# A two-layer encoder on one core: layer 0's ConvFFN in five groups, half of layer 1's W_out split where it is used, more blocks by seven products

## The chip, the core and the metric

The kernel runs on one core of one Trainium2 chip. The metric is the device time in microseconds of one execution of the whole program. Of the kernel before there are three runs, and one more execution that the hardware profiler recorded.

A core has five engines that run side by side, each through its own list of instructions in order, and that wait for one another by semaphores. PE (TensorE) multiplies matrices, and loads the stationary operand beforehand (PEld). DVE (VectorE) and ACT (ScalarE) do elementwise work, POOL (GpSimd) a little more of it, and SP issues the DMA transfers.

## The reference, cut to what matters

x has 512 positions and 1024 channels, in float32. Each of two layers has a mixing half (a Fourier group and windowed attention, joined by `w_o`) and a ConvFFN with 2816 hidden channels.

```python
mix = jnp.concatenate([rmsnorm(y_f, g_fourier_out[l]), rmsnorm(y_a, g_attn_out[l])], axis=-1)
x = x + mix @ w_o[l]

h = rmsnorm(x, norm2[l])
up = dwconv_centred(h @ w_up[l], conv_w[l], conv_b[l])
gate, val = up[..., :D_FF], up[..., D_FF:]
x = x + (jax.nn.silu(gate) * val) @ w_down[l]
```

`dwconv_centred` is a convolution over three neighbouring positions, channel by channel.

## The kernel before

**Layout and arithmetic.** x lies transposed in eight tiles of 128 channels by 512 positions. A float32 operand of a matmul is split into two halves of a reduced type: `split` lets ACT copy the high half and DVE subtract it from the source, which gives the low half (`wsplit` does it for weights, into the tiles whi and wlo, five buffers of each). `mm3` multiplies high by high, low by high and high by low, so a block product is three matmuls (L124, L125, L126). PSUM has eight banks, shared out by tags.

**The ConvFFN.** The 2816 hidden channels are 22 blocks, `fi` from 0 to 21. A *pair* is the gate block and the value block of one fi. There are two ways to make it. `up_eight` multiplies the eight input tiles one after the other: 2 blocks x 8 products, each of 512 columns. `up_seven` treats two output blocks, the two halves of the input channels and the two halves of the positions as a 2 x 2 matrix of blocks and forms it by seven products in place of eight (Strassen's scheme), each over four tiles and 256 columns. It needs four sums of weight tiles on DVE (into the tile sums and in place in wraw), seven splits in place of four, and more additions of results; the sums of the input are made once a layer (`seven_h`, into the tiles room). `SEVEN[l]` lists the fi that go this way. Then `conv` (one ACT and two DVE instructions a block), silu, the product of gate and value, and its split into `gu`.

**Groups.** `GROUPS[l]` cuts the 22 pairs into groups (first fi, number). When a group's pairs are done, `rows` multiplies its blocks by the fitting slice of W_down: eight output rows m, each with a load, a split, its matmuls in one PSUM bank, and an addition of the result to x on DVE (the *eviction*). These eight rows are a generator that the next group's pairs draw from, spread out by the rule on `want`; the rest is drained at the group's end. In the last group two of the eight rows are held back to stand behind its last pair. A group of more than four loads W_down row by row and splits it in two parts; a smaller one loads two rows at once and splits each in one.

**Prepared weights.** While layer 0's ConvFFN runs, `presplit(1)` prepares weights of layer 1: it loads a piece, folds it if it belongs to the Fourier group (keys u and f), splits it, and stores both halves in DRAM (`kept`); `PIECES[fi]` says how many pieces are drawn at each pair. Layer 1's first half fetches the halves with `fetch`. There are 44 pieces: 16 of W_qkv, 8 of W_in's Fourier columns, 4 of the Fourier weight, 16 of W_out.

**W_out.** `w_o` has two halves of eight blocks, the Fourier group's (half 0) and the attention's (half 1). The products of half 0 are placed among the last attention steps (`issue_after` with `steps`). Layer 0 loads and splits W_out on the spot (`wchunks`), layer 1 fetches both halves.

**The order.** The program is written out once, unrolled; the framework's scheduler then fixes the order on each engine, drawing instructions forward where their operands allow. So instructions of a pair, of the rows and of the pieces are interleaved on DVE and ACT.

Of the kernel before, what the change touches and what calls it, by code (L numbers as in the profile page):

```python
# [16 lines left out]
P = 128  # L17
# [15 lines left out]
RATE, STEP0 = 1, 12  # L33
FFN_BANKS = ("mm", "mm", "mm", "av", "sc", "sc")

GROUPS = ([(0, 4), (4, 4), (8, 4), (12, 3), (15, 3), (18, 4)], [(0, 4), (4, 6), (10, 6), (16, 6)])

PIECES = [1, 1, 2, 1, 2, 2, 2] + [1, 3] * 7 + [3]
SEVEN = ((7, 9, 11, 13, 15, 17, 19), (7, 8, 10, 11, 12, 14, 15, 16, 18, 19, 20, 21))


def encoder_kernel(tc, t):
# [47 lines left out]
    def halves(z):  # L90
        return [z[:, s, :] for s in range(2)]
# [63 lines left out]
    def presplit(l):  # L155

        late = []

        def keep(key, src):
            n = src.shape[-1]  # L160
            two = [temp(n, "tA", F32R) for _ in range(2)]
            with tc.issue_after(pace[0]) if pace[0] is not None else nullcontext():
                act(two[0], src)
            tt(two[1], src, f(two[0]), ALU.subtract)
            kept[key] = [dp.tile([P, n], F32, tag=f"{key}{s}", name=nm("kept")) for s in range(2)]
            store()
            late.append(lambda: [nc.sync.dma_start(o, f(z)) for o, z in zip(kept[key], two)])

        def store():
            while late:  # L170
                late.pop()()

        def cols(src, n, step):
            def load():
                raw = temp(1024, "m4")
                nc.sync.dma_start(raw[:, :n], src)
                return [raw[:, c:c + step] for c in range(0, n, step)]
            return load

        def prepare(kind, raw):  # L180
            if kind == "u":
                return fold_wu(raw)
            return fold_wf(raw) if kind == "f" else raw

        jobs = []
        for grp in (1, 0):
            for kk in range(KT // 2):
                jobs.append((cols(t["w_qkv"][l, grp, kk], 768, 384), [f"qkv{grp}{2 * kk + i}" for i in range(2)]))
        for kk in range(KT // 2):
            jobs.append((lambda kk=kk: load_wu(l, kk, temp(1024, "m4")), [f"u{2 * kk + i}" for i in range(2)]))  # L190
        for j in range(NF):
            jobs.append((lambda j=j: [load_wf(l, j, temp(1024, "m4"))], [f"f{j}"]))
        for half in range(2):
            for mp in range(KT // 2):
                jobs.append((cols(t["w_o"][l, half, :, mp * 1024:(mp + 1) * 1024], 1024, 512),
                             [f"o{half}{2 * mp + i}" for i in range(2)]))
        got = jobs[0][0]()
        for n, (_, keys) in enumerate(jobs):
            for i, key in enumerate(keys):
                keep(key, prepare(key[0], got[i]))  # L200
                if i == len(keys) - 1 and n + 1 < len(jobs):
                    got = jobs[n + 1][0]()
                yield
        store()
        while True:
            yield
# [282 lines left out]
    for l in range(L):  # L489
# [327 lines left out]
            return o  # L817

        def wo(half, mp):
            if l:  # L820
                return [fetch(f"o{half}{2 * mp + i}") for i in range(2)]
            return wchunks(t["w_o"][l, half, :, mp * 1024:(mp + 1) * 1024], 1024)

# [25 lines left out]
        def rows(f0, nf, gu):  # L849

            last = f0 + nf == FT
            for m in range(KT):
                if nf > 4:
                    w = wchunks(t["w_down"][l, m, :, f0 * P:(f0 + nf) * P], nf * P, step=nf * P // 2)
                else:
                    if m % 2 == 0:
                        raw = wtile()[:, :2 * nf * P].rearrange("p (m c) -> p m c", m=2)
                        nc.sync.dma_start(raw, t["w_down"][l, m:m + 2, :, f0 * P:(f0 + nf) * P].rearrange("m p c -> p m c"))
                    w = [wsplit(raw[:, m % 2, :])]
                kw = -(-nf // len(w))  # L860
                nh = 2 if last and l == L - 1 and m == KT - 1 else 1
                for h in range(nh):
                    q0, q1 = h * S // nh, (h + 1) * S // nh
                    nps[0] += 1
                    o = psum(FFN_BANKS[nps[0] % len(FFN_BANKS)])[:, q0:q1]
                    for k in range(nf):
                        mm3(o, [z[:, (k % kw) * P:(k % kw + 1) * P] for z in w[k // kw]],
                            [gu[k][:, s, q0:q1] for s in range(2)],
                            k == 0, k == nf - 1)
                    tt(x[m][:, q0:q1], x[m][:, q0:q1], o, ALU.add)  # L870
                    if last and l == L - 1:
                        nc.sync.dma_start(t["out"][m, :, q0:q1], x[m][:, q0:q1])
                if last and l < L - 1:
                    nxt.append(norm_tile(m, g1[:, l + 1, :], acc))
                yield

        down = iter(())
        for f0, nf in GROUPS[l]:
            gu = []

            todo = KT - 2 if f0 + nf == FT else KT
            done = 0
            for fi in range(f0, f0 + nf):
                ys_ = []
                for z, u in enumerate((up_seven if fi in SEVEN[l] else up_eight)(l, fi, h2, ts, rb2)):
                    ys_.append(conv(l, fi + z * FT, u))

                    n = 2 * (fi - f0) + z
                    want = -(-todo * (n + 2 - n % 2) // (2 * nf)) if n % 2 or n == 0 else done
                    if nf <= 4:  # L890
                        want = done + -(-(todo - done) // (2 * nf - n))
                    for _ in range(want - done):
                        next(down, None)
                    done = want
                if fi in (3, 4):
                    ts.append(seven_h(len(ts), h2, room))
                for _ in range(PIECES[fi]):
                    next(ahead)
                act(ys_[0], ys_[0], AF.Silu)
                tt(ys_[0], ys_[0], ys_[1], ALU.mult)  # L900
                c = fi % (12 if l else 8)
                if c < 4:
                    a = pair("slab")
                elif c < 8:
                    if c % 2 == 0:
                        two = temp(2048, "pT", F32R).rearrange("p (n s q) -> p n s q", n=2, s=2)
                    a = two[:, c % 2]
                else:
                    a = pair("m4")
                split(a[:, 0, :], a[:, 1, :], ys_[0])  # L910
                gu.append(a)
            for _ in down:
                pass
            down = rows(f0, nf, gu)
# [95 lines left out]
```

## Time and profile before

| | |
|---|---|
| median of three runs | 1039.85 us |
| lowest and highest | 1039.72 and 1041.09 us |
| the profiled execution's own time | 1039.14 us |
| its span, first to last instruction | 1037.4 us |
| PE, DVE, ACT busy | 1024.4, 862.5, 545.8 us |
| DMA | 140.15 MB, 42% of 16 engines' time |

The profiled execution is 1.7 us longer than its span; what lies around the span belongs to no engine's instructions. By the stretches of the trace, layer 0's mixing half fills the first 150 us, its ConvFFN lasts to about 520 us, layer 1's mixing half to about 655 us, and its ConvFFN the rest.

How to read the rows: a row of the timeline begins with start and duration, in us, then the engine, the line in the code, the operation, the tiles it writes and reads (buffer numbers left out), their shape, and how many such instructions the row merges. A row of a group has, behind the bar, busy time in us and the mean duration of one in ns, then idle time of that engine ahead of it. A row of the waits has the total in us, how many, and the longest. On DVE and ACT an instruction can begin before the one ahead of it has ended, so that a distance of starts is shorter than a duration. In a fence, a line of three dots marks rows left out.

### The profile page before, as it was taken

Reading aid. Unit: us, or ns where it says so; the run is one execution under the profiler, and the core shown is the slowest. Engines: PE = TensorE matmul, PEld = TensorE weight load, DVE = VectorE, ACT = ScalarE, POOL = GpSimd, SP = SyncE. Lnnn points to the kernel's source line nnn. Section 1 sums busy time; section 2 is a strip of 40 time slices with the busy share of each in tenths; the row PEclk is TensorE's granted clock in tenths of the full one; section 3 lists DMA queues with packets and bytes.
Section 4 is the critical chain, followed back from the end, with each engine's and each line's share of the span. In section 5 each row is a group of like instructions: output and inputs, shape, how many; then the busy total and the mean of one; then the engine's idle time right before and its main releaser. Section 6 shows DMA issues by size and latency. Waiting matters only on the chain.

```text
span 1037.4 us, 16244 instructions
## 1 busy us (share of the span) xinstructions
PE 1024.4 (99%) x5774; PEld 891.1 (86%) x5774; DVE 862.5 (83%) x1747; ACT 545.8 (53%) x1068; POOL 60.6 (6%) x142
## 2 busy tenths in 40 slices
PE   8999999999999999999999999999999999999998
PEld 8887778888888888888899887888888898989987
DVE  8788749799998889999759876396999998999973
ACT  5338736455555455555544595254555555555631
POOL 0004410000000000000000063000000000000000
PEclk9999999999999999999999999999999999999999
DMA  7232122355564546567766422423224232333242
GB/s 275 87 106 72 44 91 82 117 172 179 163 206 145 193 175 204 186 221 231 240 212 200 151 62 84 141 82 102 82 73 137 82 107 85 104 112 101 68 149 85
DMA packets 62341, 140.15 MB, mean 135 GB/s; under 512 B 6450, under 2 KB 20018, under 8 KB 62260
## 3 DMA queue, kind: packets, MB, share of 16 engines
q1 hardware_dynamic: 62260, 139.12, 41.9%
q8 instruction: 45, 0.74, 0.3%
q14 instruction: 36, 0.29, 0.1%
HBM read 116.02 MB, written 23.07 MB: 134 GB/s over the span
## 4 chain that ended last, share of the span: by engine, by line
PE 92%; DVE 5%; ACT 1%; DMA 1%; issue 1%; POOL 0%; DVEq 0%; ACTq 0%
PE ps L124 27%; PE ps L126 27%; PE ps L125 27%; PE ps L122 3%; PE ps L680 2%; PE ps L673 2%; PE ps L661 1%; DVE tF L100 1%; DMA wraw<-in_w_up_dram 1%; DVE wlo L97 1%; DVE tA L665 1%; PE ps L242 1%; PE ps L235 1%; PE ps L621 0%; PE ps L282 0%
## 5 line engine op out<-in xcount | busy, mean ns | idle before, releaser
L94 ACT ACTIVATE whi<-wraw 128x512 fp32r<-128x512 f32 (+1 forms) x323 | 190.7, 603 | 222.2 <-PE ps L126 130.5
L97 DVE TENSOR_TENSOR wlo<-wraw,whi 128x512 fp32r<-128x512 f32 (+1 forms) x331 | 213.1, 657 | 48.6 <-ACT whi L94 47.7
L124 PE MATMUL ps<-act,whi 128*128 128x512 f32 (+1 forms) x692 | 244.9, 355 | 0.0
L125 PE MATMUL ps<-act,wlo 128*128 128x512 f32 (+1 forms) x692 | 244.4, 355 | 0.4 <-DVE wlo L97 0.3
L126 PE MATMUL ps<-act,whi 128*128 128x512 f32 (+1 forms) x692 | 244.1, 354 | 0.0
L125 PEld LDWEIGHTS ps<-act,wlo 128*128 128x128 f32 x692 | 130.6, 189 | 19.4 <-DVE wlo L97 0.9
L124 PEld LDWEIGHTS ps<-act,whi 128*128 128x128 f32 x692 | 130.6, 189 | 18.7
L126 PEld LDWEIGHTS ps<-act,whi 128*128 128x128 f32 x692 | 130.7, 189 | 18.0
L100 DVE SCALAR_TENSOR_TENSOR tF<-tF,pb,tF 128x511 f32<-128x511 f32 x176 | 130.2, 747 | 4.8 <-ACT tF L94 4.6
L97 DVE TENSOR_TENSOR x<-x,ps 128x512 f32<-128x512 f32 (+1 forms) x97 | 64.9, 677 | 34.9 <-PE ps L126 34.5
L124 PE MATMUL ps<-slab,whi 128*128 128x512 f32 (+1 forms) x240 | 93.1, 390 | 0.7 <-ACT whi L94 0.7
L125 PE MATMUL ps<-slab,wlo 128*128 128x512 f32 (+1 forms) x240 | 91.8, 383 | 0.0
L94 ACT ACTIVATE tF<-tF,pb 128x512 f32<-128x512 f32 x88 | 71.1, 810 | 37.7 <-DVE tF L97 37.1
L126 PE MATMUL ps<-slab,whi 128*128 128x512 f32 (+1 forms) x240 | 89.7, 384 | 0.0
L124 PE MATMUL ps<-room,whi 128*128 128x256 f32 x266 | 75.6, 284 | 0.5 <-DVE tF L97 0.2
L125 PE MATMUL ps<-room,wlo 128*128 128x256 f32 x266 | 75.0, 282 | 0.0
L126 PE MATMUL ps<-room,whi 128*128 128x256 f32 x266 | 74.9, 282 | 0.0
L97 DVE TENSOR_TENSOR tF<-ps,rb 128x512 f32<-128x512 f32 (+1 forms) x85 | 52.6, 627 | 15.3 <-ACT rb L94 11.0
L124 PE MATMUL ps<-pT,whi 128*128 128x512 f32 (+1 forms) x148 | 56.9, 384 | 0.0
L125 PE MATMUL ps<-pT,wlo 128*128 128x512 f32 (+1 forms) x148 | 56.8, 384 | 0.0
L126 PE MATMUL ps<-pT,whi 128*128 128x512 f32 (+1 forms) x148 | 56.1, 384 | 0.0
L124 PEld LDWEIGHTS ps<-slab,whi 128*128 128x128 f32 x240 | 45.1, 188 | 9.8 <-ACT whi L94 0.9
(206 smaller groups left out, 1923.9 us busy)
## 6 DMA issues: line engine op xcount, KB each, us to landing
wraw<-in_w_up_dram SPq DMA_DIRECT2D x88, 512.0 KB, 3.8
kept<-tA SPq DMA_DIRECT2D x56, 256.0 KB, 3.2
wraw<-in_w_down_dram SPq DMA_DIRECT2D x32, 384.0 KB, 3.8
wraw<-in_w_down_dram SPq DMA_DIRECT2D x20, 512.0 KB, 4.0
whi<-kept SPq DMA_DIRECT2D x28, 256.0 KB, 3.1
wlo<-kept SPq DMA_DIRECT2D x28, 256.0 KB, 3.0
kept<-tA SPq DMA_DIRECT2D x32, 192.0 KB, 1.9
wraw<-in_w_o_dram SPq DMA_DIRECT2D x8, 512.0 KB, 4.3
```

The lines of the kernel that those rows point to most:

```text
L94: return nc.scalar.activation(out, in_, func, **kw)
L97: return (eng or nc.vector).tensor_tensor(out, a, b, op=op)
L100: return nc.vector.scalar_tensor_tensor(out=out, in0=a, scalar=s, in1=b, op0=op0, op1=op1)
L122: nc.tensor.matmul(out, a[0], b[0], start=start, stop=stop, **kw)
L124: nc.tensor.matmul(out, a[0], b[0], start=start, stop=False, **kw)
L125: nc.tensor.matmul(out, a[1], b[0], start=False, stop=False, **kw)
L126: nc.tensor.matmul(out, a[0], b[1], start=False, stop=stop, **kw)
L235: nc.tensor.matmul(pt[:, 2 * b:2 * b + 2], acc[:, b * P:(b + 1) * P], ones2, start=True, stop=True)
L242: nc.tensor.matmul(pt[:, b * P:(b + 1) * P], r[:, b:b + 1].to_broadcast([P, P]), ident, start=True, stop=True)
L661: nc.tensor.matmul(sc[:, :n], qT[p][:, e, i * P:(i + 1) * P], kT[g][:, s, j0 * P:(j1 + 1) * P], start=s == 0, stop=s == 1)
L673: tr = nc.tensor.transpose(pp[:, j * P:(j + 1) * P], pr[:, j * P:(j + 1) * P], ident)
L680: pv = nc.tensor.matmul(py[64 * e:64 * e + 64, i0 * P:(i1 + 1) * P], vp[:, j, 64 * g:64 * g + 64], pT[:, half, e, b0:b0 + 2 * (i1 - i0) + ...
```

## The change

Four tables and the places that read them change. Layer 0 has five groups in place of six, 4, 5, 4, 5 and 4 pairs. Its pairs by seven products are 7, 9, 11, 13, 14, 16, 18, 19 and 21, nine in place of seven; layer 1's are 7, 8, 9, 11, 12, 13, 14 and 16 to 21, thirteen in place of twelve. `presplit` prepares half 1 of W_out alone, 36 pieces, and `PIECES` is drawn up anew; layer 1 loads and splits half 0 of W_out where it uses it, as layer 0 does. W_down of a larger group is cut after three blocks, so five blocks are split as 384 and 256 columns. A group of five needs five places for `gu` beside the other group's four: two pT tiles of 2560 columns are taken at once at the cycle's fifth pair and hold two pairs each, and both halves of the fifth split between their last 512 columns; `gu` is now a list of two views.

```diff
-GROUPS = ([(0, 4), (4, 4), (8, 4), (12, 3), (15, 3), (18, 4)], [(0, 4), (4, 6), (10, 6), (16, 6)])
-
-PIECES = [1, 1, 2, 1, 2, 2, 2] + [1, 3] * 7 + [3]
-SEVEN = ((7, 9, 11, 13, 15, 17, 19), (7, 8, 10, 11, 12, 14, 15, 16, 18, 19, 20, 21))
+GROUPS = ([(0, 4), (4, 5), (9, 4), (13, 5), (18, 4)], [(0, 4), (4, 6), (10, 6), (16, 6)])
+
+PIECES = [1, 1, 1, 1, 2, 2, 2, 1, 3, 1, 2, 1, 3, 1, 1, 2, 1, 2, 1, 1, 2, 1]
+SEVEN = ((7, 9, 11, 13, 14, 16, 18, 19, 21), (7, 8, 9, 11, 12, 13, 14, 16, 17, 18, 19, 20, 21))
...
-        for half in range(2):
-            for mp in range(KT // 2):
-                jobs.append((cols(t["w_o"][l, half, :, mp * 1024:(mp + 1) * 1024], 1024, 512),
-                             [f"o{half}{2 * mp + i}" for i in range(2)]))
+        for mp in range(KT // 2):
+            jobs.append((cols(t["w_o"][l, 1, :, mp * 1024:(mp + 1) * 1024], 1024, 512),
+                         [f"o1{2 * mp + i}" for i in range(2)]))
...
-            if l:
+            if l and half:
                 return [fetch(f"o{half}{2 * mp + i}") for i in range(2)]
...
-                    w = wchunks(t["w_down"][l, m, :, f0 * P:(f0 + nf) * P], nf * P, step=nf * P // 2)
+                    w = wchunks(t["w_down"][l, m, :, f0 * P:(f0 + nf) * P], nf * P, step=3 * P)
...
-                            [gu[k][:, s, q0:q1] for s in range(2)],
+                            [z[:, q0:q1] for z in gu[k]],
...
-                c = fi % (12 if l else 8)
+                c = fi % (12 if l else 9)
+                if c == 4:
+
+                    big = [temp(2560, "pT", F32R) for _ in range(2)]
                 if c < 4:
-                    a = pair("slab")
+                    a = halves(pair("slab"))
                 elif c < 8:
-                    if c % 2 == 0:
-                        two = temp(2048, "pT", F32R).rearrange("p (n s q) -> p n s q", n=2, s=2)
-                    a = two[:, c % 2]
+                    a = [big[c // 6][:, (2 * (c % 2) + s) * 512:(2 * (c % 2) + s + 1) * 512] for s in range(2)]
+                elif l == 0:
+                    a = [z[:, 2048:2560] for z in big]
                 else:
-                    a = pair("m4")
-                split(a[:, 0, :], a[:, 1, :], ys_[0])
+                    a = halves(pair("m4"))
+                split(*a, ys_[0])
```

Lines behind L193 stand one higher in the changed kernel up to the last group of edits.

ACT's list in layer 1's attention, before. The rows with nmax are the exponentials of the scores, pT is the copy of their transposes, tF the output and the squares of the Fourier group.

```order
L94 ACTIVATE tA_6692,den_6647<-tA_6692,nmax_6646 128x385
L94 ACTIVATE accF_6775<-tF_6799 128x512
L94 ACTIVATE tA_6712,den_6645<-tA_6712,nmax_6644 128x385
L94 ACTIVATE act_6586<-ps_6460,pa 128x512
L94 ACTIVATE pT_6648<-ps_6671 128x256
L94 ACTIVATE tF_6831<-tF_6827 128x512
L94 ACTIVATE tA_6726,den_6647<-tA_6726,nmax_6646 128x385
L94 ACTIVATE tF_6855<-ps_6834,pa 128x258
L94 ACTIVATE acc_6029<-ps_6460 128x512
```

The same place now; whi from wraw is the high half of a block of W_out.

```order
L94 ACTIVATE tA_6765,den_6720<-tA_6765,nmax_6719 128x385
L94 ACTIVATE whi_7303<-wraw_7301 128x512
L94 ACTIVATE accF_6848<-tF_6872 128x512
L94 ACTIVATE tA_6785,den_6718<-tA_6785,nmax_6717 128x385
L94 ACTIVATE act_6659<-ps_6533,pa 128x512
L94 ACTIVATE pT_6721<-ps_6744 128x256
L94 ACTIVATE tF_6904<-tF_6900 128x512
L94 ACTIVATE tF_6928<-ps_6907,pa 128x258
L94 ACTIVATE tA_6799,den_6720<-tA_6799,nmax_6719 128x385
L94 ACTIVATE whi_7307<-wraw_7301 128x512
```

Two splits of W_out have come in between the exponentials; two more stand a few rows ahead of and behind these, one earlier still and three towards the attention's end.

DVE's list in layer 0, from the last results of pair 13 on, before. Pair 14 goes by eight products; its low halves, convolution steps (with pb) and evictions (x) follow.

```order
L97 TENSOR_TENSOR tF_3900<-tF_3900,ps_3898 128x256
L97 TENSOR_TENSOR tF_3900<-tF_3900,rb_1893 128x512
L97 TENSOR_TENSOR tF_3901<-tF_3901,ps_3897 128x256
L97 TENSOR_TENSOR wlo_4095<-wraw_4092,whi_4094 128x512
L97 TENSOR_TENSOR tF_3901<-tF_3901,rb_1893 128x256
L97 TENSOR_TENSOR wlo_4099<-wraw_4092,whi_4098 128x512
L100 SCALAR_TENSOR_TENSOR tF_4010<-tF_3900,pb,tF_4010 128x511
L97 TENSOR_TENSOR x_78<-x_78,ps_4020 128x512
```

The same place now, pair 14 by seven products:

```order
L97 TENSOR_TENSOR wlo_4065<-wraw_4055,whi_4064 128x512
L97 TENSOR_TENSOR tF_3862<-tF_3862,ps_3858 128x256
L97 TENSOR_TENSOR tF_3861<-tF_3861,rb_1893 128x512
L97 TENSOR_TENSOR sums_4081<-wraw_4055,wraw_4057 128x512
L97 TENSOR_TENSOR tF_3862<-tF_3862,rb_1893 128x256
L97 TENSOR_TENSOR wraw_4057<-wraw_4057 128x512
L97 TENSOR_TENSOR sums_4081<-sums_4081,wraw_4057 128x512
L100 SCALAR_TENSOR_TENSOR tF_3971<-tF_3861,pb,tF_3971 128x511
```

Three sums of weights have moved in between the last results of pair 13 and its first convolution step, and the next pair's splits stand behind them.

## The prediction

> **What bounds the kernel now.** I read the page first: the span, each engine's busy share, the granted clock, the chain that ended last.
>
> ```profile
> span 1037.4 us, 16244 instructions
> PE 1024.4 (99%) x5774; PEld 891.1 (86%) x5774; DVE 862.5 (83%) x1747; ACT 545.8 (53%) x1068; POOL 60.6 (6%) x142
> PEclk9999999999999999999999999999999999999999
> PE 92%; DVE 5%; ACT 1%; DMA 1%; issue 1%; POOL 0%; DVEq 0%; ACTq 0%
> ```
>
> The chain runs through PE for 92% of the span, at full clock. A busy PE need not be a fast one, so next come the busy times of stretches (columns: length, then PE, PEld, DVE, ACT and POOL with counts): layer 0's ConvFFN, layer 1's ConvFFN, the attention of layer 1, and the pairs 18 to 21 of layer 1.
>
> ```profile
> 156.00:494.00 338.00, 337.14 (x1773) 290.60 (x1772) 309.75 (x554) 184.09 (x322) 1.40 (x1) 1.00 0.54 176
> 676.00:1014.00 338.00, 337.36 (x1966) 299.19 (x1965) 302.15 (x525) 177.91 (x316) 1.01 (x1) 1.00 0.33 99
> 590.00:630.00 40.00, 38.66 (x291) 32.26 (x291) 33.96 (x116) 35.43 (x103) 21.88 (x51) 1.00 0.18 54
> 925.00:988.00 63.00, 62.88 (x429) 58.15 (x428) 59.44 (x106) 34.89 (x65) 0.00 (x0) 1.00 0.30 91
> ```
>
> PE lacks work for under 1 us in each ConvFFN of 338 us, while DVE is busy 92% and 89%. There, fewer PE cycles are time and DVE work is free until DVE falls behind. In the attention ACT is 89% busy and PE loses 1.3 us. PE's waits in layer 0's ConvFFN:
>
> ```profile
> PE ps L124 <- ACT whi L94: 0.7, 1, 0.7
> ```
>
> and in layer 1's:
>
> ```profile
> PE ps L125 <- DVE wlo L97: 0.3, 1, 0.3
> PE ps L124 <- DVE tF L97: 0.2, 1, 0.2
> ```
>
> **The matmuls.** A pair (gate and value of one fi) made by `up_eight` issues 2 x 8 x 3 = 48 matmuls of 512 columns; by `up_seven` 7 x 4 x 3 = 84 of 256. Three pairs change over: 144 go, 252 come. Rows of `rows` keep their number of matmuls. Two uninterrupted runs of the timeline, first and last start: 281 matmuls of 512, and 60 of 256.
>
> ```profile
> 199.82 0.48 PE L125 MATMUL ps<-act,wlo 128*128 128x512 f32 x1
> ...
> 263.41 0.39 PE L126 MATMUL ps<-slab,whi 128*128 128x512 f32 x1
> ...
> 812.42 0.28 PE L124 MATMUL ps<-act,whi 128*128 128x256 f32 x1
> ...
> 819.48 0.28 PE L126 MATMUL ps<-act,whi 128*128 128x256 f32 x1
> ```
>
> Spacing: 63.59 / 280 = 0.2271 us, and 7.06 / 59 = 0.1197 us. So 144 x 0.2271 = 32.70 us go and 252 x 0.1197 = 30.15 us come: **-2.55 us** on the engine that sets the end.
>
> [...]
>
> **What DVE pays.** Durations (column after the comma, ns), and one line of three consecutive operations:
>
> ```profile
> L97 DVE TENSOR_TENSOR wlo<-wraw,whi 128x512 fp32r<-128x512 f32 x251 | 170.3, 690 | 34.5 <-ACT whi L94 34.0
> L100 DVE SCALAR_TENSOR_TENSOR tF<-tF,pb,tF 128x511 f32<-128x511 f32 x176 | 130.2, 747 | 4.8 <-ACT tF L94 4.6
> L97 DVE TENSOR_TENSOR tF<-tF,ps 128x256 f32<-128x256 f32 x57 | 23.7, 415 | 2.7 <-PE ps L126 2.1
> L97 DVE TENSOR_TENSOR wlo<-wraw,whi 128x384 fp32r<-128x384 f32 x80 | 43.3, 553 | 14.1 <-ACT whi L94 13.7
> 776.81 1.89 DVE L97 TENSOR_TENSOR wlo<-wraw,whi 128x512 fp32r<-128x512 f32 x3
> 366.36 0.17 DVE L353 COPY tA<-m 128x2 f32<-128x2 f32 x1
> 366.42 0.76 DVE L97 TENSOR_TENSOR tA<-m 128x255 f32<-128x255 f32 x2
> ```
>
> Three in 1.89 us: spacing (1.89 - 0.69) / 2 = 0.60, 0.09 under the duration. Taken off all: 0.60 for 512 columns, 0.66 for a convolution step, 0.47 for 384, 0.33 for 256. Per pair, convolution and gating included, `up_seven` costs 14 x 0.60 + 4 x 0.66 + 5 x 0.33 = 12.7 us of DVE, `up_eight` 8 x 0.60 + 2.64 = 7.4. PE takes 84 x 0.1197 = 10.05 or 48 x 0.2271 = 10.9. An output row of four blocks costs DVE 1.20 (eviction and low half, both of 512 columns) and PE 12 x 0.2271 = 2.73; of five 1.40 and 3.41; of six 1.54 and 4.09. A folded piece of layer 1's W_in or Fourier weight costs DVE 0.08 + 0.67 + 0.60 = 1.35 (the last two rows less 0.09 each, and a low half), an unfolded piece of W_out 0.60.
>
> Layer 0: two more seven-product pairs (+10.6), eight evictions fewer (-4.8), eight pieces fewer (-4.8), sixteen low halves of 256 for eight of 512 (+0.5): +1.5 us of DVE in 338. Layer 1: +5.3. By the averages both stay under 93%, hidden behind PE. What counts is the single pair. Before, four pairs of layer 0 ask about 1 us more of DVE than PE takes: 11 and 13 (12.7 + two rows 2.4 + folded piece 1.35 = 16.45 against 10.05 + 5.46 = 15.5), 17 and 19 (with two rows of three blocks, 1.07 and 2.04 each, and a plain piece: 15.4 against 14.1). Only one made PE late, pair 13, where DVE never rests (second row: its stretch):
>
> ```profile
> 370.91 0.38 PE L124 MATMUL ps<-act,whi 128*128 128x256 f32 x1
> 371.95 0.49 PE L124 MATMUL ps<-slab,whi 128*128 128x512 f32 x1 [0.66 <-ACT whi L94]
> ...
> 362.00:373.00 11.00, 10.27 (x69) 9.10 (x68) 11.00 (x24) 7.01 (x14) 0.00 (x0) 1.00 0.44 158
> ```
>
> 1.04 us lie between starts that are 0.12 apart elsewhere: 0.92 lost, and 0.35 more one matmul later, 1.27. After, four pairs fall short again: 13, 14 and 16 (16.45 against 15.5 each), and 21 (13.3 against 10.05, with two rows of five behind it to cover). As many as before, so I take **0** for layer 0; the bounds are that none waits (-1.27) and that each costs 1.27 (+3.8). In layer 1 the pair 8, alone short before (12.7 + 1.2 against 12.8), is joined by 9; the seven-product pairs there show PE late by 0.7 us in all:
>
> ```profile
> 769.45 0.28 PE L124 MATMUL ps<-act,whi 128*128 128x256 f32 x1
> ...
> 777.04 0.28 PE L126 MATMUL ps<-act,whi 128*128 128x256 f32 x1
> ```
>
> 60 matmuls in 7.59 us against 7.06 is 0.53 of it, and the wait of 0.2 for DVE's tF, quoted above, comes in the next pair. A second short pair at the same price: **+0.7**, bounds 0 and 1.4. In the last group six such pairs follow each other instead of four behind an ordinary one, with one row each: DVE 14.24 against PE 14.14. The four lost 0.1 us of PE in 63; I take nothing more.
>
> **W_out of layer 1, first half.** Sixteen loads of prepared halves go, and so do their stores; four raw loads and eight splits come, into the attention. ACT, three splits of one kind in a row:
>
> ```profile
> 624.47 1.68 ACT L94 ACTIVATE slab<-tF 128x512 fp32r<-128x512 f32 x3
> ```
>
> PE's waits in the same attention:
>
> ```profile
> PE ps L673 <- POOL tA L670: 0.9, 1, 0.9
> PE ps L661 <- DVE nmax L665: 0.2, 1, 0.2
> ```
>
> and in layer 0's, where W_out is split on the spot already, the first and the last of eight:
>
> ```profile
> PE ps L673 <- ACT pT L94: 0.7, 1, 0.7
> ...
> PE ps L661 <- ACT m L94: 0.2, 1, 0.2
> ```
>
> A split is 1.68 / 3 = 0.56 us of ACT. By the order, four of the eight stand between the exponentials, 2.2 us on an engine 89% busy; behind each are queued the exponentials and the pT copies for which PE's transposes and products wait. Layer 0's eight waits sum to 2.5 us, layer 1's two to 1.1: 1.4 more with splits on the spot, the nearest row I have. Bounds -0.9 (the long wait goes) and +2.2; I take half the difference, **+0.8**. The loads are no worry: no wait of PE there is for a DMA.
>
> The wider buffers for `gu` cost nothing: both pT tiles are free when pair 4, 13 or 16 takes them, since the rows that read them are drained a group earlier.
>
> **Sum.** -2.55 + 0 + 0.7 + 0.8 = -1.05. The profiled execution took 1039.14 us, 1.74 over its span; it becomes 1038.1. The median of the three runs shown is 0.71 above it: 1039.85 - 1.05 = **1038.8**.
>
> **Rivals.** *The saving comes whole*: DVE's lead covers the short pairs as it did at 11, 17 and 19, and ACT's at the attention. 1039.85 - 2.55 = 1037.3. For it: three of four short pairs cost nothing. Against it: 13 and 14 are now neighbours.
>
> *DVE becomes the bound*: it enters pair 13 without a lead, and all four short pairs of layer 0 wait as 13 did (+3.8), with layer 1's +0.7 and the attention's +0.8: -2.55 + 5.3 = +2.75, 1042.6. It decides from the point where the lead before pair 13 is under the 1.9 us that 13 and 14 use up. For it: DVE at 11.00 of 11.00 us around 371. Against it: layer 0 asks only 1.5 us more of DVE overall.
>
> *Half-width matmuls lose their half price* when weights come late: at the slow run's spacing, 7.59 / 59 = 0.1286, 252 cost 32.4 and only 0.3 is saved; with both waits, -0.3 + 0.7 + 0.8 = +1.2, 1041.1. [...]
>
> **How the numbers follow.** Forecast (1038.0 to 1040.5, saving partly given back) 0.48; whole saving 0.31; DVE bound 0.16; half price lost 0.05. About 0.2% (2.1 us) is what a measurement can tell from no change: below 1037.8 faster, 0.31; above 1041.9 slower, 0.16; between, 0.53. The range from 1036.9 to 1041.4 leaves out the slow case and the edge of the fast one.
>
> **What would show it.** PE's matmuls of 256 columns should rise by 252 at a spacing of 0.12. Right if PE's waits are a few tenths near pairs 13 to 16 of layer 0 and 8 to 9 of layer 1, and if the transposes and products of layer 1's attention (L673 and L680, a line earlier there) wait about 0.8 us more for ACT or POOL in layer 1. The first rival shows no new PE wait; the second shows DVE without a pause for 30 us and PE waiting on wlo in several places. I would be wrong if a term of the order of 3 us sits where I look at nothing: between the layers, or in the last group.

## The result, and the profile after

| | before | after |
|---|---|---|
| median, lowest to highest | 1039.9 us, 1039.72 to 1041.09 (4 runs) | 1059.38 us, 1057.49 to 1060.34 (4 runs) |
| the profiled execution, its span | 1039.14, 1037.4 us | 1058.67, 1056.6 us |

The ratio is 1.0182, with an interval of 1.0169 to 1.0195: the change costs 19.5 us. The forecast was 1038.8 with a range up to 1041.4, and the rival that ended slower gave 1042.6. All four executions of the changed kernel have a mean granted clock of 0.998; the last section tells what that is and what it costs.

The page of the changed kernel: span, busy time of each engine, the granted clock, the chain that ended last.

```profile
span 1056.6 us, 16470 instructions
PE 1030.0 (97%) x5882; PEld 897.2 (85%) x5882; DVE 875.6 (83%) x1780; ACT 555.3 (53%) x1094; POOL 59.3 (6%) x142
PEclk9999999999999999999999999999999999999999
PE 77%; DVE 14%; DMA 5%; ACT 2%; issue 1%; POOL 0%; DVEq 0%; SPq 0%; ACTq 0%; POOLq 0%
```

DVE's share of the span has not moved from 83%, yet the chain runs through PE for 77% in place of 92%, through DVE for 14% in place of 5% and through DMA for 5% in place of 1%. By averages nothing is fuller; by the chain PE now waits for DVE, and DVE for loads. The waits of the changed kernel say the same (total in us, how many, the longest):

```profile
DVE sums L97 <- DMA wraw<-in_w_up_dram: 14.3, 15, 2.5
PE ps L124 <- DVE tF L97: 5.9, 8, 1.5
PE ps L125 <- DVE wlo L97: 3.3, 6, 0.9
```

and of the kernel before:

```profile
DVE sums L97 <- DMA wraw<-in_w_up_dram: 5.5, 11, 1.0
```

The sums of weights wait 14.3 us for W_up where they waited 5.5, and the two waits of PE that summed to 0.5 us, quoted in the prediction, are 9.2.

**Where the time went.** Over all matmuls of a trace I summed the distance from each start to the next, less what its width takes in an uninterrupted run (0.2271 us for 512 columns, 0.120 for 256, 0.173 for 384, 0.10 to 0.125 for the attention's narrower ones). What remains is time that PE lost, in us:

| | layer 0 mixing | layer 0 ConvFFN | layer 1 mixing | layer 1 ConvFFN |
|---|---|---|---|---|
| before | 27.1 | 2.3 | 5.8 | 2.4 |
| after | 26.9 | 9.7 | 7.3 | 15.2 |
| difference | -0.2 | +7.4 | +1.5 | +12.8 |

These sum to 21.5; with the 2.55 us that the matmuls save it is 19.0 of the 19.2 us by which the span grew. So the saving came, and the two ConvFFNs took it back eight times over. Layer 1's falls into three stretches (the place counted from the start of its ConvFFN), and these are followed through the experiments:

| us of PE lost | pairs 7 to 9 (120 to 160 us) | middle (180 to 220 us) | last group (from 240 us) |
|---|---|---|---|
| before | 1.0 | 0.0 | 0.9 |
| after | 4.3 | 3.0 | 7.4 |

**The last group, read in the trace.** First the stretch that the prediction used, now 925 to 988 us of the changed kernel (length, then PE, PEld, DVE, ACT, POOL):

```profile
925.00:988.00 63.00, 60.18 (x425) 55.83 (x424) 58.00 (x105) 34.54 (x65) 0.00 (x0) 1.00 0.32 99
```

PE rests 2.8 us, and so does DVE, 5.0 us of 63. Neither is full. A loop is the likely cause, so next comes what recurs once a pair. The timeline of DVE's first sum of each pair, 17 to 21, changed kernel (in brackets the idle time ahead of it, and for what):

```profile
929.03 0.69 DVE L97 TENSOR_TENSOR sums<-wraw,wraw 128x512 f32<-128x512 f32 x1
...
942.59 0.69 DVE L97 TENSOR_TENSOR sums<-wraw,wraw 128x512 f32<-128x512 f32 x1 [0.63 <-DMA wraw<-in_w_up_dram]
...
958.09 0.69 DVE L97 TENSOR_TENSOR sums<-wraw,wraw 128x512 f32<-128x512 f32 x1 [0.86 <-DMA wraw<-in_w_up_dram]
...
973.67 0.69 DVE L97 TENSOR_TENSOR sums<-wraw,wraw 128x512 f32<-128x512 f32 x1 [1.35 <-DMA wraw<-in_w_up_dram]
...
991.02 0.69 DVE L97 TENSOR_TENSOR sums<-wraw,wraw 128x512 f32<-128x512 f32 x1 [2.52 <-DMA wraw<-in_w_up_dram]
```

The distances are 13.6, 15.5, 15.6 and 17.4 us, while PE has 14.14 us of matmuls in a pair with its row. What sets them stands in the same timeline: the last low half that reads a weight tile of pair 17, SP's issue of the loads into it, and the median landing (the last number of a row of the DMA view).

```profile
938.01 0.68 DVE L97 TENSOR_TENSOR wlo<-wraw,whi 128x512 fp32r<-128x512 f32 x1
937.52 1.53 SPq L133 DMA_DIRECT2D wraw<-in_w_up_dram  x2
wraw<-in_w_up_dram SPq DMA_DIRECT2D x88, 512.0 KB, 3.7
```

There are three wraw tiles: two hold the pair's weights, one the row of W_down. The second load can go only when the low half is done, at 938.69; SP's second issue ends at 939.05, and the sum that needs it starts 3.5 us later, at 942.59. Then come all the sums, high and low halves of this pair, some 11 us with other DVE work between, and the loop closes. **In this pair load latency plus DVE's chain makes the distance, 15.5 us, and it is longer than PE's 14.14 although DVE's work alone was put at 14.24.** That the loop sets it is so far an argument from one pair; experiment 3 tests it. The same sums in the kernel before, pairs 18 to 21:

```profile
927.65 0.69 DVE L97 TENSOR_TENSOR sums<-wraw,wraw 128x512 f32<-128x512 f32 x1 [0.17 <-DMA wraw<-in_w_up_dram]
...
943.87 0.69 DVE L97 TENSOR_TENSOR sums<-wraw,wraw 128x512 f32<-128x512 f32 x1 [0.55 <-DMA wraw<-in_w_up_dram]
...
959.89 0.69 DVE L97 TENSOR_TENSOR sums<-wraw,wraw 128x512 f32<-128x512 f32 x1
...
975.54 0.69 DVE L97 TENSOR_TENSOR sums<-wraw,wraw 128x512 f32<-128x512 f32 x1 [0.59 <-DMA wraw<-in_w_up_dram]
```

Here the distances are 16.2, 16.0 and 15.7 us, no shorter, under a PE that needed 14.14 and hardly waited. DVE was busy 14.3, 15.6 and 14.8 us of the three, with waits for W_up of 0.59 us at most, so that the loop sets these distances too is not shown; that DVE was slower than PE is. So the four pairs fell behind by 1.5 to 2 us each and lived on a lead that the ordinary pair 17 had given. With six in a row the lead is gone, and PE shows it at the hand-over of its PSUM banks; the changed kernel, pair 21:

```profile
998.69 0.28 PE L126 MATMUL ps<-act,whi 128*128 128x256 f32 x1
1000.43 0.38 PE L124 MATMUL ps<-room,whi 128*128 128x256 f32 x1 [1.47 <-DVE tF L97]
```

1.74 us lie between starts that are 0.12 apart elsewhere. At 951.5, 966.8 and 982.5 us the same place lost 0.34, 0.58 and 0.95. It grows from pair to pair here, but in e2 below, whose last group has the same list, it lost 1.42, 1.21, 0.84 and 1.17: the wait recurs, its growth does not.

### The profile page after: what moved, and what is told of

The parts are those of the page before. It is cut to its first block, busy times and chain, and to the rows that moved or that the text cites. A ratio compares the mean times of both kernels' runs of the same rounds, so it can differ in the third digit from the quotient of the medians.

```text
span 1056.6 us, 16470 instructions
## 1 busy us (share of the span) xinstructions
PE 1030.0 (97%) x5882; PEld 897.2 (85%) x5882; DVE 875.6 (83%) x1780; ACT 555.3 (53%) x1094; POOL 59.3 (6%) x142
## 4 chain that ended last, share of the span: by engine, by line
PE 77%; DVE 14%; DMA 5%; ACT 2%; issue 1%; POOL 0%; DVEq 0%; SPq 0%; ACTq 0%; POOLq 0%
PE ps L124 22%; PE ps L125 22%; PE ps L126 22%; DMA wraw<-in_w_up_dram 4%; DVE wlo L97 4%; PE ps L122 3%; DVE tF L100 2%; DVE tF L97 2%; PE ps L679 2%; PE ps L672 1%; DVE sums L97 1%; DVE wraw L97 1%; PE ps L660 1%; DVE x L97 1%; ACT whi L94 1%
## 5 line engine op out<-in xcount | busy, mean ns | idle before, releaser
L94 ACT ACTIVATE whi<-wraw 128x512 fp32r<-128x512 f32 (+2 forms) x342 | 200.2, 595 | 239.0 <-PE ps L126 163.6
L97 DVE TENSOR_TENSOR wlo<-wraw,whi 128x512 fp32r<-128x512 f32 (+2 forms) x350 | 222.1, 644 | 46.4 <-ACT whi L94 45.2
L125 PE MATMUL ps<-act,wlo 128*128 128x512 f32 (+1 forms) x680 | 236.9, 350 | 1.9 <-DVE wlo L97 1.9
L124 PE MATMUL ps<-act,whi 128*128 128x512 f32 (+1 forms) x680 | 236.9, 350 | 1.1 <-ACT whi L94 1.0
L126 PE MATMUL ps<-act,whi 128*128 128x512 f32 (+1 forms) x680 | 236.2, 349 | 0.0
L124 PE MATMUL ps<-room,whi 128*128 128x256 f32 x308 | 89.0, 289 | 8.2 <-DVE tF L97 5.9
L125 PE MATMUL ps<-room,wlo 128*128 128x256 f32 x308 | 87.1, 283 | 0.5 <-DVE wlo L97 0.5
L126 PE MATMUL ps<-room,whi 128*128 128x256 f32 x308 | 86.8, 282 | 0.0
L97 DVE TENSOR_TENSOR x<-x,ps 128x512 f32<-128x512 f32 (+1 forms) x89 | 59.6, 676 | 31.7 <-PE ps L126 31.4
L124 PEld LDWEIGHTS ps<-room,whi 128*128 128x128 f32 x308 | 58.5, 190 | 12.6 <-DVE tF L97 6.5
L125 PEld LDWEIGHTS ps<-room,wlo 128*128 128x128 f32 x308 | 58.6, 190 | 1.9 <-DVE wlo L97 0.7
L126 PEld LDWEIGHTS ps<-room,whi 128*128 128x128 f32 x308 | 58.6, 190 | 0.0
L124 PE MATMUL ps<-pT,whi 128*128 128x512 f32 (+1 forms) x148 | 56.8, 385 | 0.3 <-ACT whi L94 0.3
```

The costliest lines, as they stand in the source:

```text
L94: return nc.scalar.activation(out, in_, func, **kw)
L97: return (eng or nc.vector).tensor_tensor(out, a, b, op=op)
L124: nc.tensor.matmul(out, a[0], b[0], start=start, stop=False, **kw)
L125: nc.tensor.matmul(out, a[1], b[0], start=False, stop=False, **kw)
L126: nc.tensor.matmul(out, a[0], b[1], start=False, stop=stop, **kw)
```

## The experiments

The loss by place is summed as above; "stretches" are the three of layer 1.

**1. Which part costs it.** Two kernels put back the list of seven-product pairs of one layer, one puts back both, and one makes only the change of W_out in the kernel before.

```diff
 e1: SEVEN[1] = (7, 8, 10, 11, 12, 14, 15, 16, 18, 19, 20, 21)   # as before
 e2: SEVEN[0] = (7, 9, 11, 13, 15, 17, 19)                       # as before
 e6: both
 e3, in the kernel before:
-            if l:
+            if l and half:
                 return [fetch(f"o{half}{2 * mp + i}") for i in range(2)]
```

(e3 also drops half 0 from `presplit`'s jobs.)

> The changed kernel with layer 1's list of seven-product pairs as before (twelve). PE waits for 14.7 us in layer 1's ConvFFN of the changed kernel against 1.9 before, by starts. If the thirteenth pair and the new places of the others cause them, they fall to 2 or 3 us and the time to about 1048 us (1059.4 - 12 + 0.9 for the pair given back). If they come from something else in the change (W_out split on the spot, the pT tiles taken two at a time), they stay above 10 us and the time at 1058 or more.

> The changed kernel with layer 0's list of seven-product pairs as before (seven, not nine), five groups kept. If the short pairs cause layer 0's waits (about 9.4 us by starts against 2.5 before), these fall to 2 to 4 us and the time to about 1055 us (-6 or so, +1.7 for two pairs given back). If the groups of five or the new pieces cause them, waits stay at 7 us or more and the time at 1059 to 1061.

> The kernel before with one part of the change: layer 1's first half of W_out is split where it is used. My term for it was +0.8 us (bounds -0.9 and +2.2): 1040.7 us. The changed kernel's trace suggests +1.5: 1041.4 us. A rival that puts the loss of layer 1 on this edit, by raw loads that take the buffers of the ConvFFN's first weights, expects 1045 or more.

> The changed kernel with both lists of seven-product pairs as before: what is left of the change is five groups, new pieces and W_out split on the spot. Single undoings took off 11.7 and 9.6 us; if the lists' costs add, the time is 1059.4 - 21.3 = 1038.1 us. If the two undoings share a cost (the wait of 2.5 us at 266 us stands in both), it is 1040 to 1042.

| | median, us | ratio to before | layer 0 ConvFFN | layer 1 ConvFFN | stretches |
|---|---|---|---|---|---|
| e1 | 1047.69 (2) | 1.0073 (1.0044 to 1.0103) | 9.5 | 2.8 | 1.6, 0.0, 0.7 |
| e2 | 1049.78 (2) | 1.0093 (1.0064 to 1.0123) | 3.4 | 10.9 | 2.6, 0.3, 7.5 |
| e6 | 1040.90 (8) | 1.0018 (1.0008 to 1.0028) | 3.4 | 1.0 | |
| e3 | 1040.77 (8) | 1.0009 (0.9998 to 1.0020) | 2.0 | 2.3 | |

Layer 1's list costs 11.7 us, layer 0's 9.6, and with both put back 1.0 to 1.5 us remain, of which W_out alone may be 0.85 (e3, interval -0.2 to 2.1). The two do not add: their sum is 21.3, and putting both back took off 18.5. Five groups, wider buffers for `gu` and the new PIECES change nothing that could be measured in the time (e6 against e3); by place e6 loses 1.4 us more than e3 in layer 0 and 1.3 less in layer 1. One thing in e2 needs care: layer 0's list alone also took 4.3 us off layer 1's ConvFFN, in the first two stretches. There the matmuls are the same, but the scheduler put DVE's instructions in another order. So the middle stretch, 3.0 us in the changed kernel, is not fixed by layer 1's list; the order is the likely cause. The last group's loss is the same in both, 7.4 and 7.5.

**2. Is it the thirteenth pair, or six in a row without a gap?** Same number of pairs, other places: the run of seven-product pairs lies in the third group, and 17 is ordinary again. e5 is the changed kernel with that list, e7 the kernel before with it.

```diff
 e5, e7: SEVEN[1] = (7, 8, 10, 11, 12, 13, 14, 15, 16, 18, 19, 20, 21)
```

> The changed kernel with thirteen seven-product pairs in layer 1 as well, but other ones: 9 and 17 go back to eight products, 10 and 15 change over, so that the six in a row stand in the group from 10 to 15, where eight rows of 18 matmuls lie between six pairs, and the last group has an ordinary pair at 17. If a back-to-back pair needs more than PE's own time (about 15.3 us against 10.05 + one row 4.09), a group with eight rows (10.05 + 5.45 = 15.5 a pair) hides it: waits in layer 1's ConvFFN fall from 15.2 to about 3 us and the time to 1046 to 1048. If six such pairs in a row cost the same anywhere, or a thirteenth pair does, the waits stay at 8 us or more and the time at 1052 or more.

> The kernel before with one more seven-product pair in layer 1, 13, which makes six in a row in the group from 10 to 15. PE's sum alone gives -0.85 us: 1039.0. If a run of six is covered by eight rows, 1038.5 to 1039.5; if not, each pair past the third loses about 1.2 us and the time is 1042 or more.

e5: 1047.02 us (2 runs), ratio 1.0072 (1.0051 to 1.0093), layer 1's ConvFFN 4.0, stretches 1.8, 0.3, 1.4. e7: 1039.84 us (10 runs), 1.0004 (0.9995 to 1.0014), against 1039.4 of the kernel before beside it; its ConvFFN loses 3.5 where before lost 2.4. The last pairs in e5:

```profile
925.00:988.00 63.00, 63.00 (x405) 57.54 (x405) 58.73 (x104) 34.77 (x63) 0.00 (x0) 1.00 0.34 108
```

PE does not rest at all in this window; the 1.4 us lie around it, 0.6 of them at 902 us, ahead of the last group's first sums at 912.6. Thirteen pairs are not the cost. Seven in a row, 10 to 16, are none either where eight rows of six blocks are spread over the six pairs of the third group: PE then has 10.05 + 8/6 x 4.09 = 15.5 us a pair, as long as the distance of the sums above. In the last group, with two rows held back, it has 14.14. And the one pair more in e7 saved its 0.85 us of matmuls and gave 1.1 back in layer 1's waits.

**3. The loop: take the W_down row out of the weight tiles.** Theory W: the loop over wraw sets the period. Then the rows of W_down, loaded into tA tiles that are idle there, free the third wraw for the next pair's first load, and the loss falls. Rival D: DVE's work sets it, and buffers change nothing. The edit makes two smaller transfers of one, so e11 makes the two transfers and keeps wraw.

```diff
 e4, layer 1, groups of over four:
+                    for c in (0, 3 * P):
+                        raw = temp(3 * P, "tA")
+                        nc.sync.dma_start(raw, t["w_down"][l, m, :, f0 * P + c:f0 * P + c + 3 * P])
+                        w.append(wsplit(raw))
 e11: the same two transfers into the two parts of one wraw tile
```

> The changed kernel; in layer 1 the raw rows of W_down go to the idle tA tiles, in two transfers each, so that the three wraw tiles are left to W_up. Theory W: back-to-back seven-product pairs are limited by a loop, last low half read from wraw, next load of 3.7 us, sums, splits; with more room the loads start a pair earlier, the waits in layer 1 fall from 14.7 to 6 us or less and the time to about 1050 us. Theory D: VectorE's work itself is the limit, 14.2 us a pair against PE's 14.1; waits and time stay within 2 us of 1059.4.

> Control for e4: the changed kernel, layer 1's rows of W_down loaded by two transfers as there, but into the wraw tile as before. Theory W gives nothing back, since the tiles are as scarce as before: 1058 to 1061 us, waits of 14 to 17 us. If the smaller transfers were what helped e4, 1051 to 1053.

e4: 1051.51 us (2 runs), 1.0110 (1.0081 to 1.0139), 7.9 us less than the changed kernel; layer 1's ConvFFN 9.3, stretches 4.5, 0.5, 3.9. Not all of the 7.9 is the edit's: layer 1's ConvFFN gives 5.9 of it, and layer 0, where nothing was edited, lost 7.3 in place of 9.7, since e4's execution, with a mean clock of 1.000, has no stretch at half clock there (last section). The middle stretch fell as it did in e2 without the edit, so the last group is the place to judge by. e11: 1057.82 us (2 runs), 1.0173 (1.0154 to 1.0191), stretches 4.4, 2.7, 7.4: the smaller transfers alone do nothing. DVE's first sums in e4:

```profile
951.13 0.69 DVE L97 TENSOR_TENSOR sums<-wraw,wraw 128x512 f32<-128x512 f32 x1 [0.16 <-DMA wraw<-in_w_up_dram]
...
966.16 0.68 DVE L97 TENSOR_TENSOR sums<-wraw,wraw 128x512 f32<-128x512 f32 x1
...
981.42 0.68 DVE L97 TENSOR_TENSOR sums<-wraw,wraw 128x512 f32<-128x512 f32 x1
```

The waits of 0.63 to 2.52 us for W_up are gone and the last group's loss is halved, but the distances are still 15.0 and 15.3. W holds for 3.5 us of the 7.4 in the last group; the 3.9 that are left have another cause.

**4. What is left: is it DVE's work?** From e4, two ways to give DVE less. e9 leaves a part of the computation out, the convolution's last step (the right-hand neighbour) in the value blocks of layer 1's pairs 16 to 21: six times 0.66 us. e12 gives the low halves of the last group's W_down rows to GpSimd.

```diff
 e9:
-        stt(y[:, :-1], u[:, 1:], cw[:, l, 2, m:m + 1], y[:, :-1], ALU.mult, ALU.add)
+        if not (l and m >= FT + 16):
+            stt(y[:, :-1], u[:, 1:], cw[:, l, 2, m:m + 1], y[:, :-1], ALU.mult, ALU.add)
 e12:
-                        w.append(wsplit(raw))
+                        w.append(wsplit(raw, nc.gpsimd if f0 == 10 else None))
```

> Run e4 (own buffers for W_down in layer 1) with less work for VectorE: the last convolution step is left out for the value blocks of the pairs 16 to 21 in layer 1, one instruction of 0.66 us a pair. In e4 the pairs of the last group follow each other in about 15.0 us, VectorE busy 14.5 of it, PE's own need 14.14. If VectorE's work is the limit that is left there (D, once W is lifted), the period falls by 0.5 us or more and the last group's waits from 3.5 to about 1 us: 1048.5 us or less from 1051.5. If it is the order of hand-overs between PE and ACT, nothing changes: 1051 to 1052.

> Run e4 with the low halves of W_down's rows in layer 1's last group formed by GpSimd in place of VectorE (two of 0.47 us a pair go from VectorE). D: VectorE has 13.5 us of work a pair against PE's 14.1; the last group's waits fall from 3.5 to 1.5 us or less, 1048 to 1049.5 us. A rival expects GpSimd's low halves to come too late (it took 1.36 us where VectorE worked beside it, 0.56 on the mean): PE waits on wlo and the time rises above 1052.

e9: 1051.27 us (2 runs), 1.0110 (1.0091 to 1.0128), no less than e4. By its time D falls, but the place that was edited did get faster. Its last group lost 1.7 in place of 3.9, its layer 0, where nothing was edited, 9.5 in place of 7.3: a stretch at half clock there (0.93 from 264 to 290 us), told of at the end, that e4's execution did not have. The two changes cancel. The stretch from 925 to 988 us in e4 and then, in a fence of its own, in e9:

```profile
925.00:988.00 63.00, 60.95 (x431) 57.06 (x430) 60.28 (x110) 36.13 (x67) 0.00 (x0) 1.00 0.28 93
```

```profile
925.00:988.00 63.00, 62.44 (x440) 58.49 (x440) 59.64 (x109) 36.71 (x68) 0.00 (x0) 1.00 0.32 96
```

PE works 1.5 us more of the 63. So 0.66 us a pair less of DVE's work goes with 2.2 of the 3.9 us. That DVE's work as such is the limit is not shown by it: the losses that are left in the last group of both are mostly waits for a copy on ACT, 0.5 us and three times 1.02 in e4, three times 0.44 in e9, and ACT's list changed with the edit too. Ahead of the copy at 963.90 in e4 stand a split, silu and a convolution step; ahead of the one at 965.50 in e9 the split stands behind silu. Less work and another order were not separated.

e12: 1050.73 us (2 runs), 1.0104 (1.0086 to 1.0123), last group 3.1: less than hoped, and the trace shows why. POOL's low half and DVE's sum beside it in e12:

```profile
965.55 1.02 POOL L97 TENSOR_TENSOR wlo<-tA,whi 128x384 fp32r<-128x384 f32 x1 [0.42 <-ACT whi L94]
965.74 1.39 DVE L97 TENSOR_TENSOR sums<-wraw,wraw 128x512 f32<-128x512 f32 x1
```

A sum that takes 0.69 us took 1.39 beside POOL. Between 948 and 973 us DVE was busy 24.52 us with 41 instructions, in e4 24.06 with 44: it has fewer, and they cost it more. So e12 did not give DVE less time to work, and says nothing on D.

**5. Do buffers of their own help the list that costs nothing?** e10 is e7 with e4's edit.

> The kernel before with thirteen pairs in layer 1 (as e7, 1039.8) and W_down's raw rows of layer 1 in the tA tiles (as e4). If the three wraw tiles held up the runs of pairs there too, its waits in layer 1's ConvFFN fall from 3.5 to 2 us or less and the time to about 1038.3, which beats both kernels; if not, 1039.5 to 1040.

e10: 1041.37 us (11 runs), 1.0014 (1.0005 to 1.0023), 1.5 us slower than e7 by the medians and 1.0 by the ratios, a miss. Its last group loses 2.7 against 1.5. Two waits of PE of 1.02 us each are new there, at 968.9 and 984.1. ACT and PE in e10 around the first:

```profile
967.81 0.64 ACT L94 ACTIVATE whi<-wraw 128x512 fp32r<-128x512 f32 x1 [0.24 <-PE ps L126]
968.35 0.62 ACT L94 ACTIVATE tF<-tF 128x512 f32<-128x512 f32 x1
968.87 0.80 ACT L94 ACTIVATE tF<-tF,pb 128x512 f32<-128x512 f32 x1
969.57 0.63 ACT L94 ACTIVATE tF<-ps 128x256 f32<-128x256 f32 x2
```

```profile
969.99 0.39 PE L124 MATMUL ps<-room,whi 128*128 128x256 f32 x1 [0.85 <-ACT tF L94]
```

The copy that gives PE its bank (tF from ps) stands behind silu and a convolution step on ACT, and PE waits for it. In e7 a copy stands ahead of the splits, at 968.46, and PE waits for none. The edit did relieve the loop, whose last sums are 14.5 and 15.0 us apart in e10 and 15.6 and 15.4 in e7; but PE had not been waiting for them, and the edit's new order on ACT cost it more. e4 has the same wait four times (0.5, 1.02, 1.02 and 1.02), 3.6 of the 3.9 us left in its last group.

**6. Layer 0.** e8 takes pair 14 out of the list, and so 13's neighbour.

```diff
 e8: SEVEN[0] = (7, 9, 11, 13, 16, 18, 19, 21)
```

> The changed kernel without pair 14 among layer 0's seven-product pairs, so that 13 and 16 stand alone. If the neighbours 13 and 14 made PE late, layer 0's waits fall from 9.7 us by the 2.5 us at 380 to 387, to about 7, and the time by 2.5 - 0.85 to about 1057.7. If layer 0's loss is spread over the list, more goes; if it is in the groups, nothing goes and the time rises to 1060.

e8: 1055.56 us (2 runs), 1.0154 (1.0134 to 1.0174), 3.8 us less than the changed kernel by the medians. Its two runs took 1057.04 us (profiled, with a mean clock of 0.998 as in all four of the changed kernel, and 0.99 from 156 to 494 us) and 1054.07 (mean clock 1.0), so the pair to compare is the two profiled spans, 1055.2 and 1056.6: 1.4 us less, though a pair by eight products costs 0.85 us more of PE. Layer 0's ConvFFN lost 7.4 in place of 9.7, as expected, and layer 1's 1.2 less. The stretch of pairs 13 and 14, changed kernel and then e8:

```profile
362.00:390.00 28.00, 26.93 (x187) 24.53 (x186) 26.89 (x54) 15.06 (x29) 0.00 (x0) 1.00 0.54 168
```

```profile
362.00:390.00 28.00, 28.00 (x165) 24.85 (x164) 25.68 (x52) 15.41 (x28) 0.00 (x0) 1.00 0.65 207
```

PE no longer rests: the 2.5 us lost between 380 and 387 are gone. Of the remaining 7.4 us, 2.5 lie at pair 7 (266 to 269 us in the changed kernel), where every kernel with five groups has them, e2 and e6 too. The changed kernel, first ACT and then PE:

```profile
266.61 0.38 ACT L94 ACTIVATE tF<-ps 128x256 f32<-128x256 f32 x1 [2.38 <-PE ps L126]
266.89 0.62 ACT L94 ACTIVATE whi<-wraw 128x512 fp32r<-128x512 f32 x1
...
267.57 0.38 PE L124 MATMUL ps<-act,whi 128*128 128x256 f32 x1 [0.99 <-ACT whi L94]
...
269.12 0.79 PE L124 MATMUL ps<-slab,whi 128*128 128x512 f32 x1 [0.65 <-ACT whi L94]
```

ACT sat 2.38 us at a copy that needs PE's product, with the splits for PE's next products queued behind it; when the product came, PE had to wait for those splits. Two queues in order, each holding what the other wants. In the changed kernel the other places are the half clock right behind (1.4), 462 us (0.9; 1.4 around there in e8) and the last rows of W_down behind pair 21 at 522 to 525 us (1.75), which wait only when 21 is in the list. DVE and then PE in the changed kernel:

```profile
521.62 2.48 DVE L97 TENSOR_TENSOR x<-x,ps 128x512 f32<-128x512 f32 x4 [4.59 <-PE ps L126]
524.02 0.69 DVE L97 TENSOR_TENSOR wlo<-wraw,whi 128x512 fp32r<-128x512 f32 x1
...
524.76 0.50 PE L125 MATMUL ps<-slab,wlo 128*128 128x512 f32 x1 [0.91 <-DVE wlo L97]
```

These are rows of the group's own four blocks (slab). DVE sat 4.59 us at an eviction, for PE; four evictions then ran ahead of the low half that PE wanted next. It is pair 7's knot again, with DVE in ACT's place.

## Why the prediction was wrong, step by step

**Matmuls, -2.55: right.** The records of 256 columns went from 1984 to 2236, the 252 that were counted. The sum of the losses less 2.55 meets the span within 0.3 us. e7 measures the same price apart: one more pair, 1.7 us more of PE lost, 0.9 more of span. The half-width matmuls kept their half price, 0.119 us between starts in the changed kernel too (eleven distances from 816.54 to 817.85 us); that rival is out.

**W_out in layer 1's attention, +0.8: the size fits, the mechanism does not.** e3 alone gives 0.85 (interval -0.2 to 2.1 us), and layer 1's mixing half lost 1.5 more in the changed kernel, within the bounds. The prediction had PE's transposes and last products wait for ACT or POOL. But the long wait of L673 for POOL is gone, and it is the score products (L661, now L660) that wait for DVE's pass over the scores before (nmax); before and then after, over the whole run:

```profile
PE ps L661 <- DVE nmax L665: 0.4, 2, 0.2
```

```profile
PE ps L660 <- DVE nmax L664: 2.1, 5, 0.7
```

e3 has the latter line too, so it comes with W_out. That the sum of other waits came out near 0.8 is luck.

**Layer 0, 0 with bounds to +3.8: wrong, +7.4.** The count of short pairs was the step that failed. "As many as before" took one wait at pair 13 as the price, and let 11, 17 and 19 be free because a lead covered them. Neighbours share one lead: 13 and 14 lost 2.5 us between 380 and 387, where the kernel before lost 1.27 at pair 13, and e8 lost none there. Pair 21's "two rows of five behind it to cover" did cover it; what waited were the group's own rows behind them, 1.75 us, for low halves that stand on DVE behind four evictions. Pair 7 was not looked at; its 2.5 us come with the new groups or the new PIECES, which were not separated, by the order on ACT and PE, and no balance of DVE shows them. Some 1.4 us more are the half clock behind that wait (in the five us after it the changed kernel lost 1.5 and e2, without half clock, 0.1). The rival "DVE becomes the bound" named the lead, and a right place, but its four waits of 1.27 are not what the trace has.

**Layer 1's pairs 8 and 9, +0.7 with bounds to 1.4: place right, size wrong.** That stretch lost 4.3 in place of 1.0, so 3.3; with the same list but another order in e2, 1.6. With the list as before, in e1, it lost 1.6 in all, so the list causes most of it. A second short pair does not cost what the first did; that it starts with nothing in hand is the likely reason, but not shown. DVE was busy 33.2 of the 36 us from 780 on and waited for ACT, PE and a load, so its work is not the whole of it.

**Layer 1's last group, "I take nothing more": the step that failed most, 6.5 us.** It compared 14.24 us of DVE's work with PE's 14.14 and read "0.1 us of PE in 63" as proof that four such pairs keep up. They did not: DVE's sums were 16 us apart while PE needed 14.14. The quiet PE showed a lead being spent, and the spending was to be read in the starts of the sums in the trace of before. What the balance of work left out is the loop through the weight tiles, with a load's 3.7 us in it: e4 and e11 show that it carries 3.5 us of the loss. Of the other 3.9, e9 took away 2.2 with less DVE work and, at the same time, another order on ACT; which of the two did it stays open.

**The middle of layer 1, no term: 3.0 us.** e2 lost 0.3 there with the same list, e4 0.5, and e5 0.3 with a longer run of such pairs. So the list alone does not decide it, and the scheduler's order probably does. Which instruction matters was not tried.

The prediction gave the warning itself: it ended by naming the last group as a place where a term of 3 us would make it wrong, and then had no term there.

What stays open: how much of layer 1's 12.8 us is the list and how much the order that came with it, beyond the last group, and whether another order on ACT alone would remove the 3.6 us of e4's waits for copies. No kernel here beats the one before; e7 equals it.

## What to carry to other kernels

When work shifts to an engine that is 90% busy and hidden, don't ask whether its work per step is shorter than the other's; measure the distance between the same instruction of successive steps, with every load and buffer in the loop, and compare that with the bound engine's step. If it is longer (here 16.2, 16.0 and 15.7 us against 14.14), the quiet is a lead, and each further step in a row spends some of it, until the bound engine waits. Then ask what each in-order engine has queued ahead of the instruction that is waited for; a balance of work does not show it. Pairs that wait should be kept apart by steps in which the hidden engine gains, as e5 and e8 do.

## What the runs showed of the hardware

**Half clock after 2.5 us of waits.** In the changed kernel the granted clock is 0.5 for 3.4 us right behind the waits at pair 7, 1.15, 0.40 and 0.92 us within 2.8 us. Matmuls of 256 columns in the changed kernel there:

```profile
269.72 0.41 PE L125 MATMUL ps<-act,wlo 128*128 128x256 f32 x1
269.93 0.41 PE L126 MATMUL ps<-act,whi 128*128 128x256 f32 x1
```

and in e2 behind the same waits:

```profile
269.78 0.28 PE L125 MATMUL ps<-act,wlo 128*128 128x256 f32 x1
269.89 0.28 PE L126 MATMUL ps<-act,whi 128*128 128x256 f32 x1
```

Starts are 0.21 us apart in the one and 0.11 in the other. The stretch from 264 to 290 us, changed kernel and then e2 (the third number from the end is the clock):

```profile
264.00:290.00 26.00, 24.22 (x126) 20.89 (x125) 22.64 (x40) 12.81 (x22) 0.00 (x0) 0.93 0.52 164
```

```profile
264.00:290.00 26.00, 24.22 (x134) 20.75 (x133) 22.86 (x41) 12.86 (x22) 0.00 (x0) 1.00 0.49 164
```

PE is equally busy in both and shows 8 matmuls less in the first, at a cost of some 1.4 us (1.5 us lost against 0.1 in the five us behind the wait). The change's 19.5 us have this in them, and so have e1, e5, e8, e9 and e11 in their profiled executions (in this stretch the clock of e1 and e9 is 0.93; the mean clock of all five is 0.998); e2, e4, e6 and e12 do not (1.00 in this stretch of e2 and e6; means of 1.000 in e4 and 0.999 in e12). By the mean clock it comes in some executions and not in others of one kernel: in e6, two of eight runs had a mean clock of 0.998 and took 1042.53 and 1043.20 us, the other six 1040.66 to 1041.49. The two runs of e5, 1048.78 with a mean clock of 0.998 and 1045.26 with 1.0, differ by more than 1.4 us, so times of two runs are no finer than that here. What sets it off was not shown: e2 has the same three waits, 1.15, 0.40 and 0.92 us, and keeps the full clock.

**DVE beside POOL.** In e12 a DVE sum of 512 columns took 1.39 us beside a POOL low half of 384 columns that took 1.02 (above), in place of 0.69. From 948 to 998 us the three such sums took 1.30 us on the mean, in e4 0.69; the 14 convolution steps 0.91 and 0.75. Nine low halves went to POOL there, and DVE was busier than in e4, 49.2 us of the 50 in place of 47.7. Why was not shown.
